# A recalibrated clock model for the planner of background work, with the port that VectorE and GpSimd share

## The chip, the cores and the metric

The kernel runs on one core of one Trainium2 chip. The metric is the device time of one execution in microseconds. Engines: PE is TensorE (PEld its weight loads), DVE is VectorE, ACT is ScalarE, POOL is GpSimd, SP is SyncE, which issues the loads.

## What is computed

Two decoder layers over 256 tokens of 1024 channels, in float32, then a final RMSNorm. A layer is a half-step SwiGLU feed-forward, a token mixer with three gated branches, and a second half-step feed-forward:

```python
for l in range(DEPTH):
    h = rms_norm(x, ffn1_norm[l])
    x = x + 0.5 * swiglu(h, ffn1_w_gate[l], ffn1_w_up[l], ffn1_w_down[l])
    h = rms_norm(x, mix_norm[l])
    (u, q_b, c_kv, q_i, k_i, w_i, q_c, k_c, v_c, f_c, g_a, g_b, g_c) = jnp.split(h @ w_in[l], pts, axis=-1)
    a = s5_branch(u, ...)
    b = dsa_branch(q_b, c_kv, q_i, k_i, w_i, ...)
    c = fox_branch(q_c, k_c, v_c, f_c + fox_b_f[l])
    merged = (jax.nn.sigmoid(g_a) * (a @ w_branch_ssm[l]) + jax.nn.sigmoid(g_b) * (b @ w_branch_dsa[l])
              + jax.nn.sigmoid(g_c) * (c @ w_branch_fox[l]))
    x = x + merged @ w_out[l]
    h = rms_norm(x, ffn2_norm[l])
    x = x + 0.5 * swiglu(h, ffn2_w_gate[l], ffn2_w_up[l], ffn2_w_down[l])
return rms_norm(x, final_norm)
```

The S5 branch is a diagonal complex scan; DSA is attention over the 64 keys of each query with the highest index score; fox is attention with a forget bias, the running sum of a log-sigmoid. DSA and fox have six heads of 64.

## The kernel before, in words

**Main stream.** All large products read weights once, from 415 units of at most two blocks of 128 rows by 512 columns. SP loads a unit into `raw` (4 buffers), ACT rounds it into `hi`, and DVE (or POOL, in the mixer) writes `lo = raw - hi`, the split that keeps float32 accuracy. The product is then three passes on PE: hi and lo of the weights with hi and lo of the activations (`h0h`, `h0l`, `h1h`, `h1l`, or `ath`, `bh` and so on). A unit of 512 columns is 12 matmuls. `weights` (L352) hands out units, and `feed` (L286) decides how far ahead the splits are issued.

**Background work.** Everything small (transposes of activations, the index scores and their top-k, the two attentions, the scan, the preparation of constants) is written as Python generators that yield at points where they would wait. While the program is built, `tick` (L294) is called after every few matmuls of the main stream; it lets the generator with the lowest rank go on for one step if what it waits for is ready by a model of the engines' clocks. So the order in which instructions stand on each engine is fixed at build time, by that model. On the chip each engine runs its instructions in that order and waits for semaphores.

The model is the class `Clock` (L123). `put` (L135) adds an operation to its engine: it starts when the engine is free and its inputs are done, and lasts `cost` (L150). `tick` asks it three things: whether the awaited tile is ready half a microsecond before PE's time (EAGER), whether DVE and ACT are no more than BACKLOG = 1.25 us ahead of PE, and whether a PSUM bank is free. `feed_lo` (L333) gives a split to POOL when DVE is more than 1.0 us ahead of PE and POOL less than 1.5 us (SPILL), in the mixer alone. `finish` (L306) is the other way in which background work is laid out: where the main stream needs a generator's result, all that is left of it is issued there, with no matmul of the main stream between.

**The mixer** (`mix`, L668). Units in order: index and latent columns and u; the value columns with the forget logits (390 columns); q and k of fox (256 columns a pass); q of DSA (384); then the list ORDER: gates of DSA (two halves), fox (two halves), ssm (first half), then the branch products, DSA's first. Background: `indexer` (L803) makes the index scores from `qk`, eight rounds of MAX and MATCH_REPLACE, the mask `madd`, and then attends with `qbT` and `kdT`; `latent` normalizes the latent (`cn`); `ssm` does the scan (`u`, `xt`, `t`, `w`, `g`, `state`, `y`, `vT`); `forget` (L974) runs a polynomial over 12 columns (`ft`), sums it over the tokens (`cum`), writes it to DRAM and spreads it over the partitions (`fm`); `fox` (L1020) starts when that is done. `attend` (L907) does three pairs of heads: two scores (`kdT,qbT` or `kcT,qcT`), a reduction on DVE into `st` and `mn`, exponentials on ACT with row sums `rs`, a reciprocal `ri`, scaling of `st` on ACT or DVE, transposes of `st` on PE (3 of 128x128 a head), a copy into `pt`, the value product (`pt,vd` or `pt,vs`), and its halves `bh` (ACT) and `bl` (DVE), which the branch product reads.

Every instruction is recorded through one helper, so nearly all rows of the profile have its line, L193; after the change that line is L214.

## Time and profile before

| | |
|---|---|
| median of 3 runs | 1224.71 us (1224.34 to 1225.38) |
| profiled execution | 1230.51 us, span of its instructions 1228.7 us |
| busy of the span | PE 1177.6 us (96%), DVE 804.6 (65%), ACT 601.8 (49%), POOL 197.9 (16%) |
| granted TensorE clock | 0.979 of full |
| read from HBM | 205.91 MB, 168 GB/s over the span |

PE is busy in nearly all of the span, so the rest of it, some 51 us, and the time at a lowered clock are what an order of the instructions can win or lose. A matmul's row shows its duration with the pipeline's drain (0.39 us for 512 columns); the distance from one start to the next is what a stream of them costs. A bracket behind a row gives the idle time of that engine just before it, and whose instruction ended it.

### The profile page before, as it was taken

The page shows a single profiled execution, that of the slowest core. Times are in us where ns is not written, and L with a number is a line of the kernel's source. Part 1 is how long each engine was busy: PE and PEld are TensorE (multiplying, and loading weights), DVE is VectorE, ACT ScalarE, POOL GpSimd, SP SyncE. Part 2 cuts the span into 40 slices and gives each one's busy share as a digit, 9 for nine tenths or more (in the row PEclk, how much of TensorE's full clock was granted, in tenths as well). Part 3 has the DMA queues.
Part 4 walks back from the last instruction along what each step waited for, and adds up shares of the span by engine and source line. Part 5 has one row for each costly group of instructions (what it writes and reads, how often), then busy time and mean ns, then how long its engine had stood idle before and what let it go on. Part 6 is the DMA issues. An engine that isn't in the chain of part 4 may idle for free.

```text
span 1228.7 us, 16525 instructions
## 1 busy us (share of the span) xinstructions
PE 1177.6 (96%) x5976; PEld 986.1 (80%) x5976; DVE 804.6 (65%) x1335; ACT 601.8 (49%) x883; POOL 197.9 (16%) x192
## 2 busy tenths in 40 slices
PE   5999999997999999999999999998899999999996
PEld 4887888896868788888888888888777778888885
DVE  6987555699656775555576655557985576555554
ACT  4444444643665464444455445445365545544442
POOL 4116000153401380000000000012450130000000
PEclk8999999898999999999999999999899999999998
DMA  7765465444435656647655656554543455665661
GB/s 238 219 186 166 142 217 165 142 138 128 147 103 175 200 182 188 188 121 241 189 177 168 176 155 213 188 151 130 163 146 106 145 192 179 202 185 166 197 191 67
DMA packets 114898, 208.07 MB, mean 169 GB/s; under 512 B 7454, under 2 KB 26544, under 8 KB 114816
## 3 DMA queue, kind: packets, MB, share of 16 engines
q1 hardware_dynamic: 113024, 202.80, 53.1%
q0 software_dynamic: 1504, 3.81, 1.1%
q8 instruction: 47, 0.77, 0.3%
q10 hardware_dynamic: 288, 0.39, 0.1%
q14 instruction: 35, 0.29, 0.1%
HBM read 205.91 MB, written 1.07 MB: 168 GB/s over the span
## 4 chain that ended last, share of the span: by engine, by line
PE 85%; DVE 10%; ACT 2%; issue 1%; DMA 1%; SPq 0%; DVEq 0%; ACTq 0%
PE ps_acc L193 78%; PE ps_t L193 7%; DVE lo L193 2%; DVE score L193 2%; DVE gate L193 1%; DMA raw<-in_ffn_w_gate_dram 1%; DVE ft L193 1%; DVE m L193 1%; ACT u L193 1%; ACT hi L193 1%; DVE state L193 1%; ACT vT L193 0%; DVE rsqt L193 0%; DVE g L193 0%; SPq L193 0%
## 5 line engine op out<-in xcount | busy, mean ns | idle before, releaser
L193 ACT ACTIVATE hi<-raw 128x1024 fp32r<-128x1024 f32 (+3 forms) x415 | 410.9, 991 | 467.7 <-PE ps_acc L193 397.3
L193 DVE TENSOR_TENSOR lo<-raw,hi 128x1024 fp32r<-128x1024 f32 (+4 forms) x381 | 445.6, 1173 | 291.0 <-PE ps_acc L193 245.3
L193 PE MATMUL ps_acc<-hi,h0h 128*128 128x512 f32 (+3 forms) x544 | 218.1, 401 | 5.7 <-ACT hi L193 5.6
L193 PE MATMUL ps_acc<-lo,h0h 128*128 128x512 f32 (+3 forms) x544 | 210.0, 386 | 6.7 <-DVE lo L193 6.7
L193 PE MATMUL ps_acc<-hi,h0l 128*128 128x512 f32 (+3 forms) x544 | 209.7, 385 | 0.0
L193 PE MATMUL ps_acc<-hi,h1h 128*128 128x512 f32 (+3 forms) x544 | 209.6, 385 | 0.0
L193 PE MATMUL ps_acc<-hi,h1l 128*128 128x512 f32 (+3 forms) x544 | 204.8, 376 | 0.0
L193 PE MATMUL ps_acc<-lo,h1h 128*128 128x512 f32 (+3 forms) x544 | 204.7, 376 | 0.0
L193 PE MATMUL ps_acc<-hi,ath 128*128 128x512 f32 x352 | 138.0, 392 | 0.0
L193 PE MATMUL ps_acc<-hi,atl 128*128 128x512 f32 x352 | 137.1, 390 | 0.0
L193 PE MATMUL ps_acc<-lo,ath 128*128 128x512 f32 x352 | 137.0, 389 | 0.0
L193 PEld LDWEIGHTS ps_acc<-lo,h0h 128*128 128x128 f32 x544 | 106.0, 195 | 24.7 <-DVE lo L193 7.9
L193 PEld LDWEIGHTS ps_acc<-hi,h0h 128*128 128x128 f32 x544 | 105.8, 195 | 24.2 <-ACT hi L193 6.2
L193 PEld LDWEIGHTS ps_acc<-hi,h0l 128*128 128x128 f32 x544 | 105.8, 194 | 20.1 <-DVE h0l L193 0.6
L193 PEld LDWEIGHTS ps_acc<-hi,h1h 128*128 128x128 f32 x544 | 103.2, 190 | 19.7 <-issue 2.6
L193 PEld LDWEIGHTS ps_acc<-hi,h1l 128*128 128x128 f32 x544 | 103.0, 189 | 18.2
L193 PEld LDWEIGHTS ps_acc<-lo,h1h 128*128 128x128 f32 x544 | 103.2, 190 | 17.1 <-issue 0.5
L193 POOL TENSOR_TENSOR lo<-raw,hi 128x1024 fp32r<-128x1024 f32 (+3 forms) x34 | 72.9, 2154 | 193.7 <-PE ps_acc L193 99.3
L193 PEld LDWEIGHTS ps_acc<-hi,atl 128*128 128x128 f32 x352 | 66.1, 188 | 13.9
L193 PEld LDWEIGHTS ps_acc<-lo,ath 128*128 128x128 f32 x352 | 66.1, 188 | 13.3
L193 PEld LDWEIGHTS ps_acc<-hi,ath 128*128 128x128 f32 x352 | 66.1, 188 | 13.3
L193 POOL DMA_DIRECT2D wuk<-in_dsa_w_uk_dram x4 | 2.2, 560 | 459.6 <-PE ps_acc L193 358.4
(281 smaller groups left out, 1360.1 us busy)
## 6 DMA issues: line engine op xcount, KB each, us to landing
raw<-in_ffn_w_down_dram SPq DMA_DIRECT2D x88, 512.0 KB, 4.2
raw<-in_ffn_w_up_dram SPq DMA_DIRECT2D x80, 512.0 KB, 3.6
raw<-in_ffn_w_gate_dram SPq DMA_DIRECT2D x79, 512.0 KB, 3.6
raw<-in_w_in_dram SPq DMA_DIRECT2D x56, 512.0 KB, 3.5
raw<-in_w_out_dram SPq DMA_DIRECT2D x16, 512.0 KB, 3.8
raw<-in_ffn_w_gate_dram SPq DMA_DIRECT2D x18, 256.0 KB, 2.8
raw<-in_ffn_w_up_dram SPq DMA_DIRECT2D x16, 256.0 KB, 2.8
raw<-in_w_in_dram SPq DMA_DIRECT2D x16, 256.0 KB, 2.8
```

Source lines behind the costliest of these rows:

```text
L193: return f(*args, **kw)
```

## The change

Only the model's numbers change, and one rule is added to it:

- `cost`: other durations for each class of operation. On PE a float32 product of activations gets a sum of a fixed part and a rate in place of four or two passes; a large matmul gets 0.0135 us plus columns / 2400. On ACT the fixed part is 0.2 us in place of 0.05. On DVE it is 0.155 in place of 0.07, the fast rate applies only above 128 columns, and the scan has a rate of its own. On POOL copies are dearer and memsets cheaper.
- `shared` and `held`: an operation on DVE that has two inputs in SBUF, or is a plain copy or scaling within SBUF, and every operation on POOL but a memset, use one port. If such an operation of the other engine is under way in the model, `put` lets this one start when that one ends. The last nine intervals of each engine are kept.

```diff
--- before.py
+++ after.py
@@ -128,12 +128,19 @@
         self.t = dict.fromkeys(("pe", "dve", "act", "pool", "dma"), 0.0)
         self.done = {}
 
+        self.held = {"dve": [], "pool": []}
+
     def ready(self, ap, eng=None):
         t, by = self.done.get(ap.tensor.name, (0.0, eng))
         return t + (SAME if by == eng else LATENCY)
 
-    def put(self, eng, cost, outs, ins):
+    def put(self, eng, cost, outs, ins, shared=False):
         start = max([self.t[eng]] + [self.ready(x, eng) for x in ins])
+        if shared:
+            for a, b in self.held["pool" if eng == "dve" else "dve"]:
+                if a <= start < b:
+                    start = b
+            self.held[eng] = self.held[eng][-8:] + [(start, start + cost)]
         self.t[eng] = start + cost
         for x in outs:
             done = start + cost + (1.8 if eng == "dma" else 0)
@@ -154,18 +161,31 @@
         if eng == "pe":
             if op == "transpose":
                 return 0.107
-            return ((4 if aps[1].shape[0] > HD else 2) if aps[1].dtype == F32 else 1) * max(n / 2380, out.shape[0] / 1200)
+            if aps[1].dtype == F32:
+                return (1 if aps[1].shape[0] > HD else 0.5) * (0.01 + max(n, out.shape[0]) / 600)
+            return 0.0135 + max(n / 2400, out.shape[0] / 1200)
         scalars = sum(x.shape[1:] == (1,) or list(x.shape[1:]) == [1] for x in aps[2:])
         if eng == "act":
-            return 0.05 + n / 1200 + 0.045 * scalars + (0.13 if "accum_out" in kw else 0)
+            return 0.2 + n / 1205 + 0.03 * scalars
         if eng == "pool":
-            return 0.14 + n * (2.15e-3 if op == "tensor_tensor" else 3.4e-3 if scalars else 1.15e-3)
+            return 0.16 + n * (2.2e-3 if op == "tensor_tensor" else 3.4e-3 if scalars else 0.8e-3 if op == "memset" else 2e-3)
         if op == "tensor_tensor_reduce":
             scalars = 0
         if op in ("max", "match_replace"):
             n = max(x.shape[-1] for x in aps)
-        fast = op in ("tensor_scalar", "tensor_copy", "memset") and not any("ps_" in x.tensor.name for x in aps)
-        return 0.07 + n * (0.52e-3 if fast else 1.04e-3) + 0.06 * scalars
+        if op == "tensor_tensor_scan":
+            return 0.155 + n * 2e-3
+        fast = op in ("tensor_scalar", "tensor_copy", "memset") and not any("ps_" in x.tensor.name for x in aps) and n > 128
+        return 0.155 + n * (0.52e-3 if fast else 1.04e-3) + (0.06 * scalars if n > 16 else 0)
+
+    @staticmethod
+    def shared(eng, op, aps):
+
+        if eng == "pool":
+            return op != "memset"
+        ins = [x for x in aps[1:] if "ps_" not in x.tensor.name and x.shape[1:] != (1,) and list(x.shape[1:]) != [1]]
+        fast = op in ("tensor_scalar", "tensor_copy") and len(ins) == len(aps) - 1 and "ps_" not in aps[0].tensor.name
+        return eng == "dve" and (fast or len(ins) > 1)
 
 
 class Engine:
@@ -189,7 +209,8 @@
                 outs = aps[:1] + [x for k, x in kw.items() if k == "accum_out"]
                 if op == "tensor_tensor_reduce":
                     outs.append(aps[-1])
-                self.clock.put(self.name, Clock.cost(self.name, op, aps[0], aps, kw), outs, aps[1:])
+                self.clock.put(self.name, Clock.cost(self.name, op, aps[0], aps, kw), outs, aps[1:],
+                               Clock.shared(self.name, op, aps))
             return f(*args, **kw)
 
         return call
```

How the order moves. Names: `ps_acc` are the accumulators of the main stream, `ps_t` the scratch banks of background products.

PE, first mixer, at the first DSA scores (`kdT,qbT`). Before:

```order
L193 MATMUL ps_acc<-h1h,lo 128x256
L193 MATMUL ps_t<-u_2154,xt 128x64 x4
L193 MATMUL ps_acc<-hi,h0h 128x512
L193 MATMUL ps_acc<-lo,h0h 128x512
L193 MATMUL ps_acc<-hi,h0l 128x512
L193 MATMUL ps_t<-kdT,qbT 128x256 x2
L193 MATMUL ps_t<-kdT,qbT 128x128 x2
L193 MATMUL ps_t<-ident,ft_2378 6x128 x2
```

And now:

```order
L214 MATMUL ps_acc<-hi,h1h 128x512
L214 MATMUL ps_acc<-lo,h1h 128x512
L214 MATMUL ps_acc<-hi,h1l 128x512
L214 MATMUL ps_t<-kdT,qbT 128x256 x2
L214 MATMUL ps_t<-kdT,qbT 128x128 x2
L214 MATMUL ps_t<-u_2154,xt 128x64 x4
L214 MATMUL ps_acc<-hi,h1h 128x512
```

Three matmuls of the DSA gate's first half stood ahead of these scores, now 42 do. Two groups of `u,xt` just ahead of them are now behind them, and the transposes of the forget row (`ft`) come 126 matmuls of the main stream further on.

DVE, first mixer, at the scaling of DSA's queries (`qbT`), which those scores read. Before:

```order
L193 MAX m_2663<-score 128x8
L193 MATCH_REPLACE score<-m_2663,score 128x256
L193 SCALAR_TENSOR_TENSOR ft_2382<-ft_2382,ft_2381 128x12
L193 TENSOR_SCALAR madd<-score 128x384
L193 SCALAR_TENSOR_TENSOR ft_2382<-ft_2382,ft_2381 128x12 x4
L193 TENSOR_TENSOR qbT<-ps_acc,rb 128x512
L193 TENSOR_TENSOR qbT<-ps_acc,rb 128x256
L193 TENSOR_TENSOR lo<-raw,hi 128x1024
```

And now:

```order
L214 TENSOR_TENSOR lo<-raw,hi 128x1024
L214 SCALAR_TENSOR_TENSOR ft_2299<-ft_2299,ft_2298 128x12
L214 MAX m_2667<-score 128x8
L214 MATCH_REPLACE score<-m_2667,score 128x256
L214 TENSOR_TENSOR qbT<-ps_acc,rb 128x512
L214 TENSOR_TENSOR qbT<-ps_acc,rb 128x256
L214 SCALAR_TENSOR_TENSOR ft_2299<-ft_2299,ft_2298 128x12
L214 MAX m_2694<-score 128x8
```

The scaling stood behind all sixteen pairs of MAX and MATCH_REPLACE and the mask; now six pairs and the mask are behind it, and two more splits (`lo`) ahead of it.

PE, first mixer, where the fox branch needs its input. Before, the last of fox stands in the gate of the ssm branch, with four units and a quarter still ahead of the fox branch's product:

```order
L193 MATMUL ps_t<-ident,st 128x128 x3
L193 MATMUL ps_acc<-hi,h0h 128x512
L193 MATMUL ps_acc<-lo,h0h 128x512
L193 MATMUL ps_acc<-hi,h0l 128x512
L193 MATMUL ps_t<-pt,vs 64x256 x2
L193 MATMUL ps_t<-pt,vs 64x128 x2
L193 MATMUL ps_acc<-hi,h0h 128x512
```

And now:

```order
L214 MATMUL ps_acc<-hi,bl 128x512
L214 MATMUL ps_t<-ident,st 128x128 x3
L214 MATMUL ps_t<-pt,vs 64x256 x2
L214 MATMUL ps_t<-pt,vs 64x128 x2
L214 MATMUL ps_t<-ident,st 128x128 x6
L214 MATMUL ps_t<-pt,vs 64x256 x2
L214 MATMUL ps_t<-pt,vs 64x128 x2
L214 MATMUL ps_t<-kcT,qcT 128x256 x2
L214 MATMUL ps_t<-kcT,qcT 128x128 x2
L214 MATMUL ps_t<-ident,st 128x128 x6
L214 MATMUL ps_acc<-hi,bh 128x512
```

Five sets of transposes, three value products (the third, like the second, follows its six transposes) and the last scores now stand together between the DSA branch (`hi,bl` above) and the fox branch (`hi,bh` below). Ahead of the DSA branch four sets of transposes and two value products (`pt,vd`) stand together in the same way. The second mixer has the same order.

## Rows read from the trace of the kernel before

**Rows 1.** The page's busy tenths of PE, span in 40 slices.

```profile
PE   5999999997999999999999999998899999999996
```

**Rows 2.** Who PE waited for: total us, times, longest.

```profile
PE ps_t L193 <- DVE qbT L193: 9.8, 2, 6.1
...
PE ps_t L193 <- ACT qk L193: 5.0, 2, 2.5
...
PE ps_t L193 <- DVE cn L193: 3.5, 2, 1.9
```

**Rows 3.** Windows, both parts of both mixers: width, busy us of five engines, clock, DMA.

```profile
231.63:305.64 74.01, 61.88 (x397) 56.38 (x396) 66.48 (x153) 32.62 (x61) 25.52 (x15) 0.88 0.42 131
305.64:376.78 71.14, 68.87 (x372) 54.11 (x371) 41.95 (x99) 42.67 (x91) 16.13 (x12) 0.98 0.44 135
...
832.93:903.03 70.10, 60.68 (x398) 55.46 (x396) 63.12 (x153) 32.61 (x61) 25.48 (x15) 0.90 0.44 137
903.03:974.15 71.12, 68.86 (x372) 54.10 (x371) 42.07 (x99) 42.67 (x92) 16.13 (x12) 0.98 0.43 136
```

**Rows 4.** Windows at half clock in the first parts.

```profile
238.60:245.40 6.80, 5.78 (x24) 5.39 (x25) 2.84 (x6) 2.90 (x5) 0.00 (x0) 0.50 0.02 6
286.50:296.50 10.00, 6.99 (x22) 5.37 (x23) 9.76 (x26) 2.56 (x9) 3.39 (x3) 0.50 0.43 145
...
842.90:846.10 3.20, 3.20 (x11) 3.20 (x11) 3.20 (x6) 1.06 (x1) 0.00 (x0) 0.50 0.03 4
883.80:893.90 10.10, 6.93 (x22) 5.31 (x23) 9.86 (x26) 2.51 (x9) 3.40 (x3) 0.50 0.42 146
```

**Rows 5.** Chain of waits, a feed-forward piece: start, us, what.

```profile
45.54 20.45 PE ps_acc L193 x90
```

**Rows 6.** Timeline of DVE, first mixer: start, us, instruction.

```profile
278.94 2.23 DVE L193 TENSOR_SCALAR ft<-ft 128x12 f32<-128x12 f32 x1
...
285.19 0.42 DVE L193 MAX8 m<-score 128x8 f32<-128x256 f32 x1
...
287.14 1.01 DVE L193 TENSOR_TENSOR qbT<-ps_acc,rb 128x512 f32<-128x512 f32 x2
```

**Rows 7.** Timeline of PE, first DSA scores; in brackets idle before and releaser.

```profile
287.88 1.65 PE L193 MATMUL ps_t<-kdT,qbT 64*128 64x256 f32 x8 [6.13 <-DVE qbT L193]
```

**Rows 8.** Timeline of POOL at the same time.

```profile
278.76 2.38 POOL L193 TENSOR_TENSOR lo<-raw,hi 128x1024 fp32r<-128x1024 f32 x1 [2.15 <-ACT hi L193]
```

**Rows 9.** Timeline of PE, small products of the first mixer.

```profile
235.50 1.04 PE L193 MATMUL ps_t<-u,xt 128*128 128x64 f32 x8
...
339.14 0.92 PE L193 MATMUL ps_t<-kcT,qcT 64*128 64x256 f32 x8
343.00 0.55 PE L193 MATMUL ps_t<-ident,st 128*128 128x128 f32 x3 [2.04 <-ACT st L193]
```

**Rows 10.** Timeline of DVE, steps of attention and a gate product.

```profile
342.01 0.42 DVE L193 TENSOR_TENSOR bl<-ps_t,bh 128x256 fp32r<-128x256 f32 x1
...
343.95 0.55 DVE L193 COPY pt<-ps_t 128x384 f32<-128x384 f32 x1
...
345.08 0.42 DVE L193 CUSTOM_DVE_ANT_0 st<-ps_t,fm 128x256 f32<-128x256 f32 x1
...
376.57 1.28 DVE L193 SCALAR_TENSOR_TENSOR gate<-gate,ps_acc 128x512 f32<-128x512 f32 x2
```

**Rows 11.** Timeline of ACT, exponentials of a head and a half of an output.

```profile
345.31 0.40 ACT L193 ACTIVATE st<-st,mn 128x128 f32<-128x128 f32 x1
...
345.69 0.51 ACT L193 ACTIVATE st<-st,mn 128x256 f32<-128x256 f32 x1
...
347.06 0.37 ACT L193 ACTIVATE bh<-ps_t 128x256 fp32r<-128x256 f32 x1
```

## The prediction

> **What bounds the kernel now.** I read the busy shares first, then who waits for whom on TensorE (PE), then windows by stage, then the timeline of the worst window. In the busy row PE is full nearly everywhere [rows 1]: the feed-forward stages and the last third of each mixer leave nothing to win, and at full clock a stage's 90 matmuls of 128x512 take 20.45 us, 0.227 us each [rows 5]. The reader should see in the list of waits that nearly all interior idle time of PE belongs to small background products of the mixers: the first DSA scores wait 9.8 us in all for qbT, the index scores 5.0 us for qk, the latent's transposes 3.5 us for cn [rows 2]. So I cut each mixer into a first part, from the first matmul of the value projection (128x390) to the first matmul of the second DSA gate half, and a second part, from there to the first matmul of the first fox branch. The windows give 74.01 and 70.10 us for the first part in layers 0 and 1, with PE busy 61.88 and 60.68; the second part takes 71.14 and 71.12 us with PE busy 68.87 and 68.86 [rows 3]. The first part is loose and its VectorE is busy 66.48 of 74 us; the second is tight on PE, and VectorE is busy only 41.95 us of it.
>
> A wait costs twice. After a long one the granted clock falls from full (2.4 GHz) to half (1.2 GHz): the windows behind the waits read 0.50 [rows 4]. The page's clock is 0.88 and 0.90 in the first parts, 0.98 in the second [rows 3]. Half of the PE time spent at half clock is lost: (5.78 + 6.99) / 2 = 6.4 us in layer 0, (3.20 + 6.93) / 2 = 5.1 us in layer 1.
>
> Why does the first part wait? The planner places qbT behind work that it believes cheap. In the timeline PE stands 6.13 us until 287.88 [rows 7] for a product that VectorE writes at 287.14, after top-k steps of 0.42 us and more, and after a 12-element scaling that takes 2.23 us [rows 6]. That scaling starts at 278.94, just after GpSimd started a split at 278.76 that lasts 2.38 us [rows 8]: VectorE is held until GpSimd is done. The old model knows neither the fixed cost of small operations nor this hold.
>
> **The change, part by part.** No operation is added or removed. Six more of the splits run on GpSimd (38 instead of 32, three more a mixer), and a few copies move between VectorE and ScalarE. What matters is the order.
>
> *First part, gain.* Two groups of u,xt, the second DSA scores, the forget transposes and the first transposes of the weights leave it; the first DSA scores move 39 large matmuls later. Without idle and half clock the first part of layer 0 is 74.01 - 12.13 - 6.4 = 55.5 us, of layer 1 70.10 - 9.42 - 5.1 = 55.6 us [rows 3, 4]. Work that leaves for the second part: one u,xt group 1.0, scores 0.9, transposes 0.5 [rows 9], 2.4 us, so 53.1 us are left. Which waits stay? For qbT: PE used to arrive at 287.88 - 6.13 = 281.75. Now it meets 39 x 0.227 = 8.9 us more ahead, two groups (2.0) less, and is earlier by the qk wait of 2.5 and the half-clock loss behind it, 2.9: about 283.2. VectorE must deliver 4 to 5 us earlier than 287.8. Six top-k pairs (two steps of up to 0.42 each [rows 6]) and the madd step no longer stand ahead of it, two splits of 1.2 more do, and the 5 us that it idled for the first index scores shrink; I take it as just in time. For qk: nine more matmuls and a u,xt group stand ahead of the scores, so zero. For cn: the order around it hardly moves, so I keep 1.8 us. First part: 54.9 us; gains 19.1 and 15.2, together 34.3 us. Ends: 53.1 us in both (gains 37.9), or half of today's loss remains (gains 11.6 + 9.8 = 21.4).
>
> *Second part, loss.* Fox cannot start before the forget row is summed and spread, and the transposes of that row now come ten weight units later. So most of the DSA output and nearly all of fox are left when their branch products ask for them, and `finish` lays them out with no large matmul between. In the new order the last DSA work (transposes, value product, transposes, value product) and, behind the DSA branch, five sets of fox transposes, three value products and one score product stand back to back on PE. Each arrow between them is a round trip through VectorE and ScalarE that PE sits out, where the old order hid it below large matmuls. From rows:
> - copy between transposes and value product: 0.55 [rows 10];
> - value product to the next transposes: bh 0.37 [rows 11], then from the start of bl at 342.01 to the transposes at 343.00, 1.0 [rows 9, 10], together 1.4;
> - scores to transposes: two reductions of at most 0.42 [rows 10], the exponentials of two heads, 2 x (0.40 + 0.51) [rows 11], then reciprocal and scaling, 1.0 - 0.42 = 0.6: 3.2;
> - the first fox scaling stands behind the gate product, 1.28 [rows 10], then part of the 0.6: 1.6.
>
> DSA: its second scaling stands behind four fox reductions (1.7), a copy and a scaling (1.15), covered by six matmuls (1.4) and transposes (0.5): 1.0; then copy, return, copy: 1.0 + 0.55 + 1.4 + 0.55 = 3.5. Fox: 1.6 + 0.55 + 1.4 + 0.55 + 3.2 + 0.55 = 7.9. Together 11.4 us a mixer. GpSimd's masks for fox fall into the DSA chain: one hold of VectorE, 2.4 [rows 8], gives 13.8. The first DSA transposes now wait for a scaling behind two splits and a scan; a like wait was 2.04 [rows 9], so 2.0. Clock: each chain leaves PE mostly idle for longer than the 6.13 us wait; the stretch behind that one had 6.99 us of PE time at half clock [rows 4], a loss of 3.5; two such, 7.0. Sum 22.8 us.
>
> The second part without idle and half clock is 71.14 - 2.27 - 0.02 x 71 = 67.5 us; 67.5 + 2.4 + 22.8 = 92.7, that is 21.6 more in each layer, 43.1 in all. Ends: the chains alone (11.4; +20.3 in all), or a third half-clock stretch and the last bh and bl of both chains on top (22.8 + 3.5 + 1.6 = 27.9; +53.3 with rounding).
>
> *The rest.* The feed-forward stages' own waits and the preparation of layer 0 move by a few matmuls under a full PE; zero, and 2 us either way if that cover fails.
>
> Net: 43.1 - 34.3 = +8.8 us. The profiled execution took 1230.5 us, 5.8 above the median of the runs; on the median the forecast is 1224.7 + 8.8 = **1233.5 us**.
>
> One rule is weighed against the trace. The row shows a whole split's length lost by an operation of 12 elements [rows 6, 8]. The Trainium skill, "SBUF — State Buffer", § "Who interferes with whom", says that whichever of the two engines issues first gets the shared pair for the whole instruction and the other fully blocks; the trace agrees (2.23 of 2.38 us). By that rule the three more splits a mixer on GpSimd cost VectorE time where they were meant to save it; were all of them in the chains, the sum would be some 9 us higher. I charge one hold, since VectorE is idle for 29 us of the second part [rows 3].
>
> **Rivals.**
> 1. *The clock holds: faster.* Place: the two forced chains. If the many small products there keep the clock full, 7.0 us a mixer fall away: 8.8 - 14 = -5.2, 1219.5 us; with better overlap down to 1207. It decides once the second part loses under 18.4 us a mixer instead of 22.8. For it: the waits for cn of some 1.8 us [rows 2] have none of the four half-clock windows [rows 4] behind them. Against: the 6.13 us wait lies under one, and the chains are sparse for longer.
> 2. *VectorE bounds the first part: slower still.* If its 66.5 and 63.1 us of busy time [rows 3] are needed whatever the order, the gains are 7.5 and 7.0 only: 43.1 - 14.5 = +28.6, 1253 us. Against: much of that busy time is holds like the one of rows 6 and 8.
> 3. *They cancel.* The gains and losses are of one size; within 2.4 us of no change by accident, 1224.7 us.
>
> **How the numbers follow.** Forecast 0.50 (its own range 1228 to 1245), rival 1 0.24, rival 2 0.13, rival 3 0.13. A measurement of this kernel can tell about 0.2%, 2.4 us. Faster 0.25, same 0.13, slower 0.62. The ends of both parts together reach from -17.6 (1207) to +32 (1257); for 8 in 10 I cut to 1217 to 1250, which takes in rival 1 and leaves out most of rival 2.
>
> **What would show it.** Right: the first part near 55 us, without the wait for qbT and with the clock near 1.0; the second near 92 us, with PE's new waits for pt, st and ri (transposes and value products) just ahead of the DSA and fox branches and windows at 0.50 there. Wrong in the first step: a wait for qbT or lo remains before the second gate. Wrong in the second: the second part under 85 us, or clock 1.0 in the chains.

## The result: 1233.45 us, 0.7% slower

The changed kernel takes 1233.45 us (median of four runs, 1231.57 to 1234.74) against 1224.64 us for the kernel before on the same chip: a ratio of 1.0070, 95% interval 1.0052 to 1.0087. The forecast was 1233.5 us. The direction and the mechanism were right; that the total came within 0.1 us is luck, since three of its terms were off and nearly cancel, as shown below. One of the eight runs of one kernel below (VectorE's costs only, 1245.76 us) counts as slow and is left out of its ratio.

The profiled execution took 1234.74 us. From the page of the changed kernel, the span and the 40-slice rows of PE and of its granted clock:

```profile
span 1233.0 us, 16530 instructions
...
PE   6999999999969999999999999999998799999996
...
PEclk8999999999989999999999999999998999999999
```

Before, the shortfalls of PE lay in slices 10 and 28 to 29 [rows 1]. Now they lie in slice 12 and in slices 31 and 32: later, in the second part of each mixer. Who PE waited for, after (total us, times, longest):

```profile
PE ps_t L214 <- ACT st L214: 13.9, 8, 3.1
PE ps_t L214 <- DVE st L214: 6.2, 6, 1.3
...
PE ps_t L214 <- DVE gate L214: 3.9, 4, 1.1
PE ps_t L214 <- DVE cn L214: 2.3, 2, 1.2
PE ps_t L214 <- ACT qk L214: 1.2, 1, 1.2
```

Against [rows 2] the wait for qbT (9.8 us) is gone, that for qk fell from 5.0 to 1.2 us, and that for `st`, the probabilities of DSA and fox, grew to 20.1 us from 4.1:

```profile
PE ps_t L193 <- ACT st L193: 4.1, 2, 2.0
```

Windows of the changed kernel, cut at the same matmuls as [rows 3], with the end of each mixer behind them (from the first fox branch to the last unit of the output projection in layer 0, and to its fourth unit in layer 1, which is why the two differ in length):

```profile
core 0: us, PE busy (x) PEld busy (x) DVE busy (x) ACT busy (x) POOL busy (x), PEclk, DMA share, GB/s
231.28:285.70 54.42, 53.21 (x376) 49.82 (x375) 50.74 (x126) 29.73 (x49) 22.02 (x12) 1.00 0.60 179
831.37:887.22 55.85, 53.44 (x377) 49.90 (x376) 50.85 (x126) 29.72 (x49) 21.94 (x12) 1.00 0.61 175
285.70:373.09 87.39, 76.90 (x394) 58.55 (x392) 56.02 (x121) 45.85 (x102) 27.08 (x20) 0.93 0.38 115
887.22:974.22 87.00, 76.13 (x394) 58.14 (x392) 55.99 (x121) 45.87 (x102) 26.97 (x20) 0.95 0.38 116
373.09:430.42 57.33, 54.70 (x255) 44.75 (x255) 39.65 (x42) 26.52 (x34) 14.80 (x9) 0.99 0.54 165
974.22:1021.72 47.50, 44.88 (x204) 36.53 (x204) 33.41 (x35) 20.76 (x25) 11.86 (x6) 0.95 0.49 156
```

The first part is 54 to 56 us at full clock with PE busy all but 1.2 to 2.4 us of it; the second part grew to 87 us with 10.5 us idle in layer 0 and the clock at 0.93. In the timeline of PE the first DSA scores now start with no wait at all, and the idle pieces stand where the groups without large matmuls are (start, us, instruction; in brackets idle before and releaser):

```profile
282.46 0.92 PE L214 MATMUL ps_t<-kdT,qbT 64*128 64x256 f32 x8
...
341.87 0.55 PE L214 MATMUL ps_t<-ident,st 128*128 128x128 f32 x3 [0.91 <-ACT st L214]
343.69 0.69 PE L214 MATMUL ps_t<-ident,st 128*128 128x128 f32 x3 [1.27 <-DVE st L214]
...
348.01 0.90 PE L214 MATMUL ps_t<-ident,st 128*128 128x128 f32 x3 [1.45 <-ACT st L214]
...
360.65 1.58 PE L214 MATMUL ps_t<-pt,vs 128*64 128x256 f32 x8
...
370.09 0.88 PE L214 MATMUL ps_t<-ident,st 128*128 128x128 f32 x6 [3.10 <-ACT st L214]
```

Windows of layer 0 at the DSA group and at the fox group, each with a few large matmuls ahead of it, and one at half clock:

```profile
334.28:352.46 18.18, 14.01 (x61) 8.90 (x60) 11.20 (x23) 8.21 (x20) 9.91 (x7) 0.77 0.31 102
357.50:373.09 15.59, 9.27 (x57) 5.74 (x54) 8.15 (x25) 6.79 (x21) 0.00 (x0) 0.95 0.10 34
...
344.20:354.20 10.00, 8.01 (x27) 4.78 (x27) 4.82 (x11) 3.65 (x8) 3.93 (x4) 0.50 0.19 72
```

All 10.5 us of idle time stand in these two: 4.2 at the DSA group and 6.3 at the fox group, where GpSimd has no work at all.

### The profile page after: what moved, and what is told of

The parts are those of the page before. It is cut to its first block, busy times and chain, and to the rows that moved or that the text cites. A ratio compares the mean times of both kernels' runs of the same rounds, so it can differ in the third digit from the quotient of the medians.

```text
span 1233.0 us, 16530 instructions
## 1 busy us (share of the span) xinstructions
PE 1181.4 (96%) x5976; PEld 986.2 (80%) x5976; DVE 805.5 (65%) x1331; ACT 601.3 (49%) x881; POOL 204.8 (17%) x198
## 4 chain that ended last, share of the span: by engine, by line
PE 86%; DVE 8%; ACT 3%; DMA 2%; issue 1%; SPq 0%; POOL 0%; ACTq 0%; DVEq 0%; POOLq 0%
PE ps_acc L214 78%; PE ps_t L214 8%; DVE lo L214 1%; DMA raw<-in_ffn_w_gate_dram 1%; DVE score L214 1%; DVE gate L214 1%; DVE vT L214 1%; ACT hi L214 1%; ACT st L214 1%; DVE w L214 1%; DVE st L214 1%; ACT u L214 1%; DMA raw<-in_ffn_w_down_dram 0%; DMA raw<-in_w_in_dram 0%; DVE rsqt L214 0%
## 5 line engine op out<-in xcount | busy, mean ns | idle before, releaser
L214 DVE TENSOR_TENSOR lo<-raw,hi 128x1024 fp32r<-128x1024 f32 (+4 forms) x375 | 439.9, 1178 | 267.9 <-PE ps_acc L214 207.7
L214 PE MATMUL ps_acc<-hi,h0h 128*128 128x512 f32 (+3 forms) x544 | 213.0, 391 | 5.9 <-ACT hi L214 5.9
L214 PE MATMUL ps_acc<-lo,h0h 128*128 128x512 f32 (+3 forms) x544 | 207.2, 381 | 5.7 <-DVE lo L214 5.7
L214 PE MATMUL ps_acc<-hi,h0l 128*128 128x512 f32 (+3 forms) x544 | 207.1, 381 | 1.2 <-DVE h0l L214 1.2
L214 POOL TENSOR_TENSOR lo<-raw,hi 128x1024 fp32r<-128x1024 f32 (+3 forms) x40 | 87.1, 2180 | 173.2 <-PE ps_acc L214 164.7
L214 PEld LDWEIGHTS ps_acc<-hi,ath 128*128 128x128 f32 x352 | 66.1, 188 | 13.2
```

The lines of the kernel that those rows point to most:

```text
L214: return f(*args, **kw)
```

## The experiments

Two theories stand against each other. **A:** the order sets the time: PE gains where qbT comes later, and loses where `finish` lays out groups of small products before the DSA and fox branches, which PE waits through at a falling clock. **B:** the loss comes from the splits on GpSimd, beside which VectorE stands. All results, sorted as told; stages are layer 0 / layer 1 of the profiled execution in us, the clock is its mean granted clock. The kernel before took 1224.6 to 1227.0 us beside them, so kernels are compared by their ratios. The expectations count twice as many splits on GpSimd as the traces have: by its rows there are 34 before and 40 in the change, where the expectations say 68 and 80, and the differences halve likewise.

| run | median us | ratio to before (95%) | first part | second part | end of mixer | clock |
|---|---|---|---|---|---|---|
| before again | one run, 1228.08 | | 71.1 / 69.2 | 71.4 / 71.3 | 55.1 / 43.8 | 0.981 |
| the change | 1233.45 | 1.0070 (1.0052 to 1.0087) | 54.4 / 55.9 | 87.4 / 87.0 | 57.3 / 47.5 | 0.984 |
| costs only | 1219.85 | 0.9951 (0.9937 to 0.9964) | 54.4 / 55.8 | 78.1 / 81.1 | 58.2 / 45.3 | 0.985 |
| port rule only | 1225.34 | 0.9994 (0.9971 to 1.0016) | 60.2 / 60.4 | 75.6 / 75.2 | 57.8 / 45.2 | 0.985 |
| VectorE's costs only | 1239.49 | 1.0068 (1.0034 to 1.0102) | 61.1 / 63.3 | 78.6 / 77.2 | 58.2 / 45.3 | 0.984 |
| before, qbT first | 1228.02 | 1.0016 (1.0005 to 1.0028) | 75.9 / 74.6 | 66.3 / 66.3 | 55.3 / 44.0 | 0.980 |
| the change, more room | 1221.60 | 0.9963 (0.9949 to 0.9977) | 64.7 / 65.7 | 69.9 / 69.9 | 56.6 / 45.2 | 0.987 |
| costs, PACE 35 | 1204.99 | 0.9824 (0.9812 to 0.9837) | 56.5 / 57.9 | 70.6 / 70.6 | 56.5 / 48.1 | 0.993 |
| the change, two splits moved | 1229.89 | 1.0024 (1.0014 to 1.0034) | 54.4 / 56.3 | 87.6 / 85.5 | 58.6 / 47.1 | 0.981 |
| the change, PACE 35 | 1252.19 | 1.0212 (1.0196 to 1.0228) | 52.4 / 52.5 | 99.2 / 98.3 | 57.6 / 47.2 | 0.973 |
| costs, PACE 35, one split more | 1211.71 | 0.9876 (0.9862 to 0.9890) | 56.5 / 58.0 | 71.2 / 70.6 | 60.8 / 49.0 | 0.989 |
| costs, PACE 32 | 1208.39 | 0.9849 (0.9836 to 0.9862) | 56.6 / 58.1 | 71.3 / 71.6 | 58.2 / 46.2 | 0.992 |
| costs, PACE 35, late merged | 1199.16 | 0.9779 (0.9756 to 0.9802) | 56.5 / 57.5 | 70.5 / 70.6 | 54.9 / 43.6 | 0.995 |

**The kernel before, profiled again** (no edit).

> The kernel before once more, for its profile. The profiled execution of before took 5.8 us more than the median of its runs, that of the changed kernel no more than its own runs. If that was one slow execution, a fresh profile comes out at 1225 +-2 us and the 3.9 us between the first parts of the two layers (74.0 and 70.1) shrinks, with the shorter half-clock stretch in layer 0. If a profile of this kernel always costs that much, it is 1230 us again with the same stretches.

It took 1228.08 us, 1.1 above the expected range, against a median of 1226.78 over 19 runs of this kernel beside it. Windows of its first parts:

```profile
231.69:302.77 71.08, 59.90 (x397) 54.83 (x396) 64.12 (x152) 32.29 (x61) 25.10 (x15) 0.90 0.45 133
830.90:900.11 69.21, 61.36 (x398) 56.15 (x397) 60.77 (x152) 32.31 (x61) 24.96 (x15) 0.90 0.47 137
```

The gap between the layers shrank from 3.9 to 1.9 us, as expected. So the 74.01 us of [rows 3] held 2.9 us that this execution doesn't show, and layer 1 another 0.9. The forecast's gain was worked out from an execution that was slow in just the place that the change mends.

**The new durations alone**, without the port rule in `put`.

```diff
-        if shared:
+        if False:
```

> The new durations without the rule on the shared ports. TensorE's order in the first part is word for word that of the changed kernel; in the second part 20 small products instead of 31 stand at the DSA branch and 24 instead of 31 before the fox branch; GpSimd keeps the same 80 splits. Theory A (the moved order sets the time: chains that TensorE waits out before the branches): first part 54 to 56 us as in the changed kernel, second part 87.2 less about a third of its 17.3 us above packed work, so 82 +-2, and 1223 us (1219 to 1227). Theory B (the loss is GpSimd's splits holding VectorE): splits as many, so 1231 to 1235 us.

1219.85 us, within A's range. The first parts are the change's to 0.1 us, the second parts 78.1 and 81.1 us where 82 +-2 was expected, with as many splits on GpSimd as the change has. The new durations are worth having, and the port rule on top of them turns a gain into a loss: the second parts are 9.3 and 5.9 us longer with it, the other stages differ by at most 2.2. This run alone does not say that the longer groups do it: the splits are as many but not the same ones. The change has those of units 114 and 115, just ahead of its DSA group, on GpSimd, this kernel has them on VectorE. The runs with two splits moved and with longer groups tell the two apart.

**The port rule alone**: `held` and `shared` as in the change, every line of `cost` as before.

```diff
-            return 0.2 + n / 1205 + 0.03 * scalars
+            return 0.05 + n / 1200 + 0.045 * scalars + (0.13 if "accum_out" in kw else 0)
...
-        return 0.155 + n * (0.52e-3 if fast else 1.04e-3) + (0.06 * scalars if n > 16 else 0)
+        return 0.07 + n * (0.52e-3 if fast else 1.04e-3) + 0.06 * scalars
```

> The rule on the shared ports with the old durations. The first product with qbT stands 2 units later than before, behind fewer rounds of the top-k on VectorE; no group of more than 8 small products stands together at a branch; GpSimd has the 68 splits of before. Theory A: the wait for qbT goes, first part 55 to 60 us, second part 71 to 76 us as nothing is forced, 1197 to 1208 us, faster than both kernels. Rival (the dearer durations alone make the room in the first part): first part over 66 us and 1220 to 1228 us.

The stages came as A said or within 0.5 us of it (60.2 and 60.4; 75.6 and 75.2), the time did not: 1225.34 us, in the range of the rival, whose first part of over 66 us did not come. I had taken the gain of the first part from the first profile of before; against the second one it is 10.9 + 8.8 = 19.7 us, less 8.1 in the second part and 4.2 at the end of the mixers, 7.4 us. The profiled execution is 8.0 us below that of before (1220.08). Its twelve runs spread from 1217.7 to 1234.2 us, and they follow the granted clock, 0.988 in the fastest and 0.970 in the slowest. Its first part has the same small products as the change's and is 5.8 us longer in layer 0; what it keeps is the wait for qk, with 6.8 us at half clock behind it:

```profile
PE ps_t L210 <- ACT qk L210: 5.0, 2, 2.5
...
231.86:292.03 60.17, 56.71 (x376) 52.38 (x375) 51.02 (x125) 29.04 (x49) 25.49 (x13) 0.94 0.52 157
```

**VectorE's new durations alone**, in the kernel before.

```diff
+        if op == "tensor_tensor_scan":
+            return 0.155 + n * 2e-3
-        fast = op in ("tensor_scalar", "tensor_copy", "memset") and not any("ps_" in x.tensor.name for x in aps)
-        return 0.07 + n * (0.52e-3 if fast else 1.04e-3) + 0.06 * scalars
+        fast = op in ("tensor_scalar", "tensor_copy", "memset") and not any("ps_" in x.tensor.name for x in aps) and n > 128
+        return 0.155 + n * (0.52e-3 if fast else 1.04e-3) + (0.06 * scalars if n > 16 else 0)
```

> The kernel before with VectorE's new durations alone. qbT comes as early on VectorE as in the changed kernel, 20 small products stand before the fox branch and none at the DSA branch, GpSimd has 84 splits (80 in the changed kernel, 68 before). Theory A: first part 54 to 57 us, second part 71 plus about 9 for the fox chain, 80 +-3, and 1214 us (1206 to 1221). Theory B (GpSimd's holds): more splits than the changed kernel, so 1231 to 1238 us.

The second part fits A (78.6 and 77.2), the first part doesn't (61 to 63 us, with a wait of 2.7 us for qk left in layer 0); the profiled execution took 1228.3 us. All eight runs lie above A's range of time, so A was wrong about the time. By the ratio the kernel takes some 1235 us, within B's range; the median of all eight, 1239.49, is 1.5 us above it. But without the slow one the runs go from 1227.2 us at a clock of 0.987 to 1241.3 at 0.977: 0.010 of some 1235 us is 12 us of full-speed work, most of the spread. Whether GpSimd's splits have a part in it this run does not show.

**qbT first, in the kernel before.**

```diff
         for rd in range(TOPK // 8):
+            if rd == 3:
+                yield lambda: self.rows_read
             for c, t, n in self.PARTS:
```

> The kernel before with its own model and two lines more: the rounds of the top-k from the fourth on wait until the scaling of qbT has been issued, so that qbT stands ahead of 10 of the 16 searches on VectorE and the first product with qbT comes at the third gate unit of the second half (it came at the end of the queries). Theory A: the waits of the first part are the place of qbT and nothing else, so the first part falls from 70 to 57 us or less (54 to 60); in the second part no group is forced, but six chains stand closer together, 71 to 80 us; 1212 us (1203 to 1222). Rival (VectorE is simply full in the first part, and whatever is put behind qbT comes back as a wait right after): first part 57 to 62, second part over 82, 1224 to 1230 us.

A was wrong here: 1228.02 us, nothing gained, though PE no longer waits for qbT. Neither theory's stages came (75.9 and 66.3 us in layer 0; more small products stand ahead of the cut between the parts), only the rival's time. First and second part together are 142.1 and 140.9 us, those of before 142.5 and 140.5. Both parts in layer 0, the timeline of PE, and windows behind the wait:

```profile
231.23:307.09 75.86, 67.85 (x435) 63.63 (x433) 59.26 (x144) 31.93 (x57) 19.08 (x14) 0.89 0.46 136
307.09:373.38 66.29, 63.44 (x335) 48.53 (x334) 49.69 (x119) 40.68 (x89) 11.33 (x9) 1.00 0.46 135
```

```profile
258.04 0.44 PE L193 MATMUL ps_t<-ident,cn 128*128 128x128 f32 x2 [3.06 <-DVE cn L193]
...
279.00 0.59 PE L193 MATMUL ps_t<-ident,ft 128*6 128x128 f32 x2 [2.20 <-DVE ft L193]
```

```profile
279.20:292.40 13.20, 13.20 (x63) 12.58 (x62) 3.19 (x5) 0.17 (x1) 4.00 (x5) 0.50 0.47 142
876.40:889.60 13.20, 13.20 (x63) 12.54 (x61) 3.21 (x5) 1.06 (x1) 4.01 (x5) 0.50 0.51 154
```

The wait for qbT (5.4 and 3.2 us in the second profile of before) is gone; those for the forget transposes (`ft`), which before had too (1.6 and 1.8 us), and for cn grew, to 2.2 and 3.1 us in layer 0. In all PE is idle 2.8 us less in layer 0 and 2.5 in layer 1. But behind the wait for `ft` 13.2 us at half clock follow, in which PE is busy throughout, 6.6 us lost for 2.2 us of waiting, and PE's busy time in both parts rises by 2.5 and 2.9 us: the clock took back what the waits gave. VectorE is full in front of that wait (busy 11.93 of the 12 us from 270 to 282). So the place of qbT alone buys nothing.

**More room for the background, with the whole new model.**

```diff
-TICK, BACKLOG, PREP, EAGER = 1.5, 1.25, 0.0, -0.5
+TICK, BACKLOG, PREP, EAGER = 1.5, 1.75, 0.0, -0.5
-FEED, PACE = 0.3, 25.0
+FEED, PACE = 0.3, 15.0
```

> The changed kernel with its two limits on the background loosened (BACKLOG from 1.25 to 1.75, PACE from 25 to 15): qbT as late as in the changed kernel, groups before the branches of 10, 4 and 10 small products instead of 24, 7 and 31, but 92 splits on GpSimd instead of 80. Theory A (the loss of the second part is the forced groups): second part 87 down to 74 to 79 us, first part 54 to 58, 1212 us (1205 to 1222). Theory B (GpSimd's holds): 12 more splits, second part 85 us or more, 1230 us or more.

1221.60 us, at the edge of A's range and far from B's, with 46 splits on GpSimd, six more than the change. The stages miss both: more small work came early, so the first part is 65 us and the second 70. Together they are 134.6 and 135.6 us against 141.8 and 142.9 for the change: the looser limits are worth 7.2 us a mixer. Two limits moved at once and other small work with them, so not all of it need be the shorter groups.

**Costs only, with PACE 35.** PACE is the model's time in us after which each further step of the state-space generator (`ssm`) counts as overdue and goes ahead of the others.

```diff
-FEED, PACE = 0.3, 25.0
+FEED, PACE = 0.3, 35.0
```

> The costs-only kernel with PACE 35 for 25, so that the state-space generator becomes urgent later and the attention generators come sooner: no group at the DSA branch, 14 small products before the fox branch (24 in costs only), the first product with qbT one unit earlier, 72 splits. Theory A: second part 79.6 less the DSA group's waits, 74 +-3, first part 55 to 59 us, 1213 us (1208 to 1219). Rival: the earlier product with qbT waits again, first part 62 us or more, 1220 to 1226 us.

1204.99 us, 1.8% faster than before and below A's range. With PACE 35 the ssm generator is overdue later, so the attentions go first; no group is forced at the DSA branch. PE's busy time in the second part is 68.6 us of 70.6, and neither part is below full clock. Its first parts:

```profile
229.78:286.31 56.53, 55.32 (x394) 51.42 (x393) 53.54 (x135) 32.40 (x58) 26.90 (x15) 1.00 0.61 176
814.80:872.65 57.85, 55.51 (x394) 51.49 (x393) 53.58 (x135) 32.19 (x58) 26.70 (x15) 1.00 0.59 170
```

They hold the forget transposes, the second DSA scores and a group of u,xt, which the change moves to the second part, and PE waits neither for `ft` nor for qbT. So a short first part doesn't need that work to leave. What this kernel, the change and costs only have in common there is that the waits for qbT are gone and those for qk nearly so (1.2 us in one layer), and with them the half clock behind. Which of the moved steps on VectorE it takes for that no run separates.

**Two splits of the change back on VectorE.** The model still books them on GpSimd.

```diff
             eng = nc.gpsimd if self.spill and ... else nc.vector
+            if i % 207 in (114, 115):
+                eng = Engine(nc.vector.eng, "pool", self.clock)
```

> The changed kernel with the splits of units 114 and 115 (and 321, 322 in the second layer) issued on VectorE instead of GpSimd, with the model told nothing, so that every engine's order is otherwise unchanged. These are the two splits beside which VectorE's instructions at the DSA branch took 1.96 and 2.87 us. Theory B (GpSimd's holds make the loss at the branch): the group at the DSA branch shortens by the 2 to 3 us of the holds, second part 84 to 85 us, 1228 us (1226 to 1230). Theory A (the group itself, small products that each wait for VectorE and ScalarE): two splits of 1.2 us each take the holds' place on VectorE, second part 86 to 88.5 us, 1233 us (1231 to 1236).

The edit moves only one of these two splits, and another one with it. GpSimd and VectorE at the DSA branch, in the change:

```profile
335.21 5.20 POOL L214 TENSOR_TENSOR lo<-raw,hi 128x1024 fp32r<-128x1024 f32 x2 [3.95 <-ACT hi L214]
```

```profile
336.21 1.96 DVE L214 SCALAR_TENSOR_TENSOR ahl<-vT,ahl 128x512 fp32r<-128x512 f32 x1 [3.85 <-ACT ahl L214]
338.10 2.87 DVE L214 TENSOR_TENSOR lo<-raw,hi 128x512 fp32r<-128x512 f32 x1
```

And VectorE and GpSimd in this run:

```profile
333.74 0.69 DVE L214 SCALAR_TENSOR_TENSOR ahl<-vT,ahl 128x512 fp32r<-128x512 f32 x1 [2.85 <-ACT ahl L214]
```

```profile
336.69 2.52 POOL L214 TENSOR_TENSOR lo<-raw,hi 128x1024 fp32r<-128x1024 f32 x1 [12.27 <-DVE ri L214]
```

The second of the two splits in the row of 335.21, beside which VectorE took 2.87 us, is unit 117 and stays on GpSimd (the row of 336.69). Moved were the first of the two and an earlier one, which started at 328.86, beside nine copies of vT that took 4.81 us on VectorE in the change and take 2.58 in this run.

It took 1229.89 us, in B's range: against the change's ratio the two splits a mixer are worth some 0.46% of 1225 us, 5.6 us (on the medians 3.6). The profiled execution doesn't show where: its second parts are 87.6 and 85.5 us, and it is the slowest of nine runs, at a clock of 0.981 where the other eight had 0.982 to 0.991. VectorE comes to the DSA group 4.8 us earlier in layer 0 (the start of bl ahead of it), but PE's idle time in the second part falls only from 10.5 to 9.8 us there and from 10.9 to 9.3 in layer 1. So GpSimd's splits have a part in the loss, 3.6 to 5.6 us for these two a mixer; which part of it is the hold itself and which the clock (0.987 in the median run, 0.984 to 0.985 in the change) stays open.

**Longer groups**: the whole change with the same edit.

```diff
-FEED, PACE = 0.3, 25.0
+FEED, PACE = 0.3, 35.0
```

> The changed kernel with PACE 35 for 25, which under the dearer model makes the forced groups longer: 47 small products at the DSA branch (24 + 7 in the changed kernel) and 38 before the fox branch (31); the first product with qbT comes after the last gate unit. Theory A: the second part's 17.3 us above packed work grow with the groups to 17.3 x 85 / 62 = 24, first part 53 (less small work in it), second part 95 (91 to 99), 1246 us (1238 to 1254). Rival (the groups are cheap, and the second part is bounded by VectorE's and ScalarE's work): second part within 2 us of 87, 1231 to 1235 us.

1252.19 us, near A's 1246 and inside its range. The wait for `st` grows from 20.1 to 32.7 us, and the second part takes 11.5 us more for 23 more small products in the groups:

```profile
PE ps_t L214 <- ACT st L214: 32.5, 12, 4.7
```

```profile
283.12:382.29 99.17, 82.91 (x410) 64.21 (x408) 50.48 (x117) 47.79 (x107) 45.76 (x29) 0.87 0.37 108
```

This kernel also has 62 splits on GpSimd, 22 more than the change, so by itself its time fits B as well. The place of the waits settles it. PE and GpSimd at the groups of layer 0:

```profile
355.38 1.54 PE L214 MATMUL ps_t<-ident,st 128*128 128x128 f32 x6 [4.41 <-ACT st L214]
```

```profile
362.81 0.71 POOL L214 DMA_DIRECT2D fm<-cumd  x1 [24.04 <-DVE mn L214]
```

GpSimd is idle for 24.04 us until 362.81, and in this time PE is idle 7.9 us inside the DSA group. Fox groups with no large matmul between show the same: PE is idle 2.0 us in one of 10 small products (costs, PACE 35), 3.2 in one of 24 (costs only), 6.3 in one of 31 (the change) and 6.7 in one of 38 (this kernel).

The same constant that gained 15 us under the new durations alone costs 19 us with the port rule (1.3% and 1.4% by the ratios).

**One split more on GpSimd, at the mixer's end**, on costs only with PACE 35.

```diff
+            if i % 207 == 133:
+                eng = Engine(nc.gpsimd.eng, "dve", self.clock)
```

> The costs-only kernel with PACE 35 (1205 us), with one split of a mixer more on GpSimd: that of unit 133 (340), which the kernel before has there and every kernel with a changed model has on VectorE, between the halves of the merged rows at the mixer's end; the order is otherwise unchanged. If this split is what lengthens the end of the mixer (56.5 and 48.1 us against 55.1 and 43.8), 1 to 1.5 us go in the first layer and up to 4 in the second, with its half-clock stretch: 1201 us (1199 to 1203.5). If it is the place of the transposes of the merged rows in TensorE's order, which comes earlier in all of them, nothing goes: 1204 to 1206 us.

Slower by 6.7 us and above both ranges, so this split on VectorE is not what lengthens the end. It shows a hold undisguised, since no other instruction moved. VectorE, GpSimd and PE in layer 0:

```profile
394.92 2.69 DVE L214 TENSOR_TENSOR gate<-gate 128x512 f32<-128x512 f32 x1
...
398.31 0.69 DVE L214 TENSOR_TENSOR gate<-gate 128x512 f32<-128x512 f32 x1
```

```profile
394.72 2.34 POOL L214 TENSOR_TENSOR lo<-raw,hi 128x1024 fp32r<-128x1024 f32 x1
```

```profile
397.66 0.33 PE L214 MATMUL ps_t<-ident,gate 128*128 128x128 f32 x1 [2.88 <-DVE gate L214]
```

The sum of two gate products takes 2.69 us beside the split and 0.69 alone, and PE waits 2.88 us for it, where it waits 0.90 without the split. Layer 1 has the same.

**Costs only, PACE 32.**

```diff
-FEED, PACE = 0.3, 25.0
+FEED, PACE = 0.3, 32.0
```

> The costs-only kernel with PACE 32: 4 and 10 small products before the last unit and the fox branch where PACE 35 has 3 and 14, the first product with qbT at the same unit, 76 splits on GpSimd instead of 72. Theory A: first part as with PACE 35, second part less about a microsecond each, 1203 us (1201 to 1207). Theory B: 4 more splits cost, 1207 to 1211 us.

1208.39 us, not the gain that A gave and inside B's range. Each part is 0.1 to 1.0 us longer than with PACE 35, with 38 splits on GpSimd instead of 36. At the ends of the mixers layer 0 takes 1.7 us more, at a clock of 0.97, and layer 1 takes 1.9 less. Why the time rises is not settled by this run.

**The merged transposes later**, on costs only with PACE 35.

```diff
         hi, lo = hT
         yield src
+        if gcol is None and hT is self.new[1]:
+            yield lambda: self.n_used % 207 > 132
```

> The costs-only kernel with PACE 35 (1205 us), where the transposes of the second merged half wait until TensorE is in the third unit of the output projection (they stand in its first; in the kernel before, in its second). In the layer-1 end of the mixer of that kernel TensorE waits 0.57 us for h0l, then 0.90 and 1.07 us for gate in front of these transposes, and the clock falls to half right behind them. If the place of these transposes is what lengthens the end of the mixer: the gate waits of 3.9 us in all go, the half-clock stretch at the end of the second layer's mixer too, 56.5 and 48.1 us become 55 and 44 to 45, and 1200 us (1197 to 1203). If the end of the mixer is late for another reason (h0l, the split of unit 133 on VectorE), the waits come back on h0l or lo: 1204 to 1207 us.

1199.16 us, 2.2% faster than before (95% interval 2.0 to 2.4%) and the fastest of all. The waits for gate, 3.9 us in all, are gone; those for h0l grew from 1.1 to 1.9 us. The gate waits stood here in the kernel that it builds on (PE, end of layer 1's mixer):

```profile
978.68 0.33 PE L214 MATMUL ps_t<-ident,gate 128*128 128x128 f32 x1 [0.90 <-DVE gate L214]
980.08 0.90 PE L214 MATMUL ps_t<-ident,gate 128*128 128x128 f32 x3 [1.07 <-DVE gate L214]
```

Its own windows, second parts and ends of the mixers, show full clock throughout:

```profile
288.05:358.59 70.54, 68.59 (x377) 54.20 (x376) 50.38 (x113) 43.34 (x96) 18.72 (x15) 1.00 0.45 139
872.70:943.25 70.55, 68.61 (x376) 54.19 (x375) 50.12 (x113) 43.72 (x96) 18.59 (x15) 1.00 0.45 141
358.59:413.46 54.87, 53.85 (x255) 44.02 (x255) 39.62 (x42) 26.62 (x34) 14.77 (x8) 1.00 0.53 173
943.25:986.88 43.63, 42.61 (x204) 34.72 (x203) 32.75 (x35) 20.39 (x24) 11.86 (x6) 1.00 0.54 171
```

## Why the prediction was right, and where it was not

| term, both layers | forecast | against the first profile of before | against the second |
|---|---|---|---|
| first part | -34.3 | -33.8 | -30.0 |
| second part | +43.1 | +32.1 | +31.7 |
| end of the mixers | 0 | +6.0 | +6.0 |
| sum | +8.8 | +4.3 | +7.6 |
| profiled executions | | +4.2 | +6.7 |
| medians | +8.8 | +8.8 | |

- **First part: right.** 54.9 us was forecast, 54.4 and 55.9 came, with the clock at 1.00, no wait for qbT, and 1.2 us for qk and 2.3 for cn left over both layers. The place of qbT alone does not do it, as the run with qbT first shows; nor does it need the forget transposes to leave, as the kernel with costs and PACE 35 shows. A wait for qk that stays, with the half clock behind it, makes the first part some 60 us (port rule only). And the base was one slow execution, so the gain was 30, not 34.
- **Second part: mechanism right, two terms too large.** The groups appeared where the order showed them. Of 87.39 us in layer 0, 69.9 are the packed and moved work of the forecast, 87.39 - 76.90 = 10.5 are idle, and 76.90 - 69.9 = 7.0 are left. That this equals the 7.0 forecast for the clock is chance: in the second part PE was busy 10.0 us at half clock in layer 0 and 8.3 in layer 1, so the clock cost 5.0 and 4.2 by the forecast's own rule. The other 2 us stand, as an estimate, in the value products: one takes 1.58 us in a group at full clock (the row of 360.65 above), and they took 0.87 among large matmuls before. The idle time was put at 15.8 (chains 11.4, hold 2.4, wait for the first DSA transposes 2.0). The last of these did not come at all, and the pieces at the DSA branch add up to 4.2 and before fox to 6.3, where 5.9 (with the hold) and 7.9 stood. The long links came as forecast (1.45 for the 1.4 from a value product to the next transposes, 3.10 for the 3.2 from scores to transposes); the copies between transposes and value product, put at 0.55 each, left at most 0.3 us of idle time, and part of them is in the longer value products.
- **"The rest" at zero: wrong, +6.0 us.** The prediction named full PE as its cover and did not look at the end of the mixer, where the model puts the transposes of the second merged half one unit earlier, right behind the gate product that they wait for. In layer 1 a half-clock stretch followed. Of the 6.0 us, 2.1 are idle time, 1.7 are that stretch, and 1.5 are half clock that the fox groups leave to the first matmuls of the fox branch. Moving the transposes two units later was tried on costs only with PACE 35, which has the same place for them, and there took all of it back (54.9 and 43.6 us); on the change itself it was not tried.
- **Net.** The second part over by 11.4, the first part over by 4.3 and the end short by 6.0 leave an error of 1.2 us in the sum of stages. That is luck. By the forecast's own account, a second part that loses 17.5 and 17.1 us a mixer, as it did, instead of 22.8 gives 8.8 - 11.0 = -2.2 us, no change; the base and the end of the mixers made up for it.
- **Rivals.** The clock did not hold in the groups (0.93 and 0.95 over the second parts), so the first fell on its mechanism, though its mark, a loss under 18.4 us a mixer, was reached, by shorter waits and a smaller loss to the clock. VectorE did not bound the first part: its busy time there went from 64.1 and 60.8 to 50.7 and 50.9 us, so a good part of it was not needed there, as argued; how much of that was holds and how much moved work no run separates.
- **The holds.** The rule of the Trainium skill, "SBUF — State Buffer", § "Who interferes with whom", that the engine that is second waits for the whole instruction, agrees with the run that has one split more at the mixer's end: the split ended at 394.72 + 2.34 = 397.06, and VectorE's sum, issued 0.2 us after it, ended 0.55 us later, where it takes 0.69. I had charged one hold of 2.4 us a mixer, beside the masks for fox. It came, at 1.2 us (2.02 against 0.81 for three like scalings later in the trace):

```profile
347.16 2.07 POOL L214 TENSOR_TENSOR fm<-fm,ccm 128x256 f32<-128x256 f32 x2 [0.94 <-DMA fm<-cumd]
```

```profile
347.56 2.02 DVE L214 TENSOR_SCALAR st<-st,ri 128x256 f32<-128x256 f32 x3
369.64 0.81 DVE L214 TENSOR_SCALAR st<-st,ri 128x256 f32<-128x256 f32 x3
```

  Ahead of the DSA group layer 0 of the change has three more, beside splits, that the forecast did not have: 2.2 us (4.81 - 2.58), 1.27 (1.96 - 0.69) and some 2. Moving two of the three splits gave 5.6 us by the ratios, 2.8 a mixer.

## What to carry to other kernels

A planner's model needn't be truer to give a better order: each half of this change alone was level or faster, both together slower, with more of the background left until a consumer forced it. So when costs are made dearer, retune the limits that gate on them (here PACE and the place of one set of transposes took the new durations from 1219.9 to 1199.2 us), but measure, since the same step of PACE cost time with the port rule; and look for groups of small products directly ahead of the instruction that needs them. Before a gain is read from one profiled execution, compare it with the timed runs and take a second profile if they differ by more than the effect.

## What was not expected of the hardware

With qbT first, waits of 2.20 and 2.03 us were each followed by 13.2 us at half clock in which PE was busy the whole time; the wait of 6.13 us [rows 7] had 10 us of half clock at its place [rows 4]. And one unchanged program's twelve runs (port rule only) went from 1217.7 to 1234.2 us with its mean granted clock from 0.988 to 0.970. The two best kernels, with hardly a wait in the mixers, stayed within 6.9 us (six runs) and 3.3 us (five) at 0.991 to 0.996. But the four runs of the change with PACE 35, with the longest waits of all, stayed within 4.4 us as well, so long waits alone do not make the spread.
